# Two-layer expert MLP: the last weight loads swapped and cut into pieces, the last two experts' layers interleaved

## The chip, the cores and the metric

The kernel runs on one core of a Trainium2 chip. The metric is the device time of one execution in microseconds (us). The profiler's page gives, beside it, the span of the profiled execution, from the first to the last recorded instruction; it is about 2 us shorter than the device time. Every time below that is taken from inside the execution counts from the start of that span.

## The reference

Eight experts each apply two matrix products with a ReLU between them to their own 256 tokens. All inputs and the output are float32.

```python
n_experts, capacity, hidden, expert_hidden = 8, 256, 512, 2048
# x  [8, 256, 512]   w1 [8, 512, 2048]   w2 [8, 2048, 512]
h = np.matmul(x, w1)
h = np.maximum(h, 0)
return np.matmul(h, w2).astype(np.float32)
```

One expert's w1 and its w2 are 4 MB each in float32, x is 0.5 MB, the output 0.5 MB.

## The kernel before, in words

The kernel goes through the experts e = 0 to 7 (line 93). For each one it has the following parts.

Loads: `load_x` (lines 57 to 60) brings x as float32 over SyncE's queue. `load_w1` (62 to 65) and `load_w2` (67 to 85) bring the weights over GpSimd's queue, and the transfer converts them to bfloat16, so each weight takes 2 MB in SBUF. w2 of expert 7 comes in six pieces, in units of one 128-row block: 4, 4, 4, 2, 1 and 1 (line 77). All other weights are one DMA each. The order on GpSimd's queue is w1 of 0, w2 of 0, w1 of 1, w2 of 1 and so on (lines 89 to 96). A load may be issued as soon as its buffer is free: w1 has four buffers (line 45), w2 four (line 46), x three (line 42).

Preparation: VectorE casts x to bfloat16 (line 101), TensorE transposes it in eight 128 by 128 blocks into one PSUM tile (line 105), and VectorE copies that to `xT` (line 107).

Layer 1: 64 matmuls of 128x128 by 128x256 (line 119). Eight of them fill one PSUM tile `h_ps`, of which there are four (line 50), and ScalarE applies the ReLU on the way to `hT` in bfloat16 (line 126). There are two `hT` buffers (line 47).

Layer 2: 32 matmuls of 128x128 by 128x512 (line 140) into two PSUM tiles `o_ps`, one for each half of the tokens. For experts 0 to 6 all 16 blocks k of the first half come before those of the second (line 138). For expert 7 the two halves alternate at each k (line 136), so that the matmuls can follow the pieces of w2 as they land. VectorE copies the result to SBUF (line 151; for the second half of expert 7 ScalarE does, line 149), and SyncE's queue stores it (line 156; lines 153 and 154 for expert 7, one store per half, on SyncE's and ScalarE's queue).

The order on each engine is chosen by a scheduler from the program and its dependences. On TensorE it came out as: layer 1 of e, layer 2 of e, transposes of e + 1, layer 1 of e + 1.

Of the kernel before, what the change touches and what calls it, by code (L numbers as in the profile page):

```python
# [1 line left out]

# [5 lines left out]

FP32 = mybir.dt.float32  # L10
BF16 = mybir.dt.bfloat16

J = 16


@with_exitstack
def kernel(
    ctx: ExitStack,  # L20
    tc: tile.TileContext,
    x: bass.AP,
    w1: bass.AP,
    w2: bass.AP,
    out: bass.AP,
):
    nc = tc.nc
    P = 128
    E, C, H = x.shape
    F = w1.shape[2]  # L30
    MC = C // P
    K1 = H // P
    K2 = F // P
    NB = K2 // J

    x_v = x.rearrange("e (p mo) k -> e p (mo k)", mo=MC)
    out_v = out.rearrange("e (p mo) k -> e p (mo k)", mo=MC)
    w1_v = w1.rearrange("e (p ko) n -> e p (ko n)", ko=K1)
    w2_v = w2.rearrange("e (b p j) n -> e p b (j n)", p=P, j=J)

    const = ctx.enter_context(tc.tile_pool(name="const", bufs=1))
    x_pool = ctx.enter_context(tc.tile_pool(name="x_pool", bufs=3))
    xb_pool = ctx.enter_context(tc.tile_pool(name="xb_pool", bufs=2))
    xT_pool = ctx.enter_context(tc.tile_pool(name="xT_pool", bufs=2))
    w1_pool = ctx.enter_context(tc.tile_pool(name="w1_pool", bufs=4))
    w2_pool = ctx.enter_context(tc.tile_pool(name="w2_pool", bufs=4))
    hT_pool = ctx.enter_context(tc.tile_pool(name="hT_pool", bufs=2))
    out_pool = ctx.enter_context(tc.tile_pool(name="out_pool", bufs=3))
    psum_t = ctx.enter_context(tc.tile_pool(name="psum_t", bufs=1, space=bass.MemoryType.PSUM))
    psum_h = ctx.enter_context(tc.tile_pool(name="psum_h", bufs=4, space=bass.MemoryType.PSUM))  # L50
    psum_o = ctx.enter_context(tc.tile_pool(name="psum_o", bufs=3, space=bass.MemoryType.PSUM))

    identity = const.tile([P, P], BF16, name="identity")

    xs, w1s, w2s = {}, {}, {}

    def load_x(e):
        t = x_pool.tile([P, MC * H], FP32, name="x_sb")
        nc.sync.dma_start(t[:], x_v[e])
        xs[e] = t  # L60

    def load_w1(e):
        t = w1_pool.tile([P, K1 * F], BF16, name="w1_sb")
        nc.gpsimd.dma_start(t[:], w1_v[e])  # L64
        w1s[e] = t

    def load_w2(e):

        t = w2_pool.tile([P, NB, J * H], BF16, name="w2_sb")
        w2s[e] = []  # L70
        if e < E - 1:
            nc.gpsimd.dma_start(t[:], w2_v[e])  # L72
            for b in range(NB):
                for j in range(J):
                    w2s[e].append(t[:, b, j * H:(j + 1) * H])
        else:
            pieces = [4, 4, 4, 2, 1, 1]
            k = 0
            for i, n in enumerate(pieces):
                b, j = divmod(k, J)  # L80
                c = w2_pool.tile([P, n * H], BF16, name=f"w2_last{i}", bufs=1)
                nc.gpsimd.dma_start(c[:], w2_v[e, :, b, j * H:(j + n) * H])  # L82
                for q in range(n):
                    w2s[e].append(c[:, q * H:(q + 1) * H])
                k += n

    load_x(0)
    load_x(1)
    load_w1(0)
    make_identity(nc, identity)  # L90
    load_w2(0)

    for e in range(E):
        if e + 1 < E:
            load_w1(e + 1)
            load_w2(e + 1)
        if e + 2 < E:
            load_x(e + 2)

        xb = xb_pool.tile([P, MC, P, K1], BF16, name="xb")  # L100
        nc.vector.tensor_copy(xb[:].rearrange("p m q k -> p (m q k)"), xs[e][:])  # L101
        xt_ps = psum_t.tile([P, K1, MC, P], BF16, name="xt_ps")
        for ko in range(K1):
            for mo in range(MC):
                nc.tensor.transpose(xt_ps[:, ko, mo, :], xb[:, mo, :, ko], identity[:])  # L105
        xT = xT_pool.tile([P, K1, C], BF16, name="xT")
        nc.vector.tensor_copy(  # L107
            xT[:].rearrange("p k c -> p (k c)"),
            xt_ps[:].rearrange("p k m q -> p (k m q)"),
        )  # L110

        w1_r = w1s[e][:].rearrange("p (ko b q j) -> p ko b q j", ko=K1, b=NB, j=J)
        hT = hT_pool.tile([P, K2, C], BF16, name="hT")
        for pr in range(K2 // 2):
            h_ps = psum_h.tile([P, 2, C], FP32, name="h_ps")
            for s in range(2):
                b, j = divmod(pr * 2 + s, J)
                for ko in range(K1):
                    nc.tensor.matmul(  # L119
                        h_ps[:, s, :],  # L120
                        w1_r[:, ko, b, :, j],
                        xT[:, ko, :],
                        start=(ko == 0),
                        stop=(ko == K1 - 1),
                    )
            nc.scalar.activation(  # L126
                hT[:, pr * 2:pr * 2 + 2, :].rearrange("p a c -> p (a c)"),
                h_ps[:].rearrange("p a c -> p (a c)"),
                mybir.ActivationFunctionType.Relu,
            )  # L130

        last = e == E - 1
        out_sb = out_pool.tile([P, MC, H], FP32, name="out_sb")
        o_ps = [psum_o.tile([P, H], FP32, name="o_ps") for _ in range(MC)]
        if last:
            order = [(k, m) for k in range(K2) for m in range(MC)]
        else:
            order = [(k, m) for m in range(MC) for k in range(K2)]
        for k, m in order:
            nc.tensor.matmul(  # L140
                o_ps[m][:],
                hT[:, k, m * P:(m + 1) * P],
                w2s[e][k],
                start=(k == 0),
                stop=(k == K2 - 1),
            )
            if k == K2 - 1:
                if last and m == 1:
                    nc.scalar.copy(out_sb[:, m, :], o_ps[m][:])  # L149
                else:  # L150
                    nc.vector.tensor_copy(out_sb[:, m, :], o_ps[m][:])  # L151
                if last:
                    eng = nc.scalar if m == 1 else nc.sync
                    eng.dma_start(out_v[e, :, m * H:(m + 1) * H], out_sb[:, m, :])
        if not last:
            nc.sync.dma_start(out_v[e], out_sb[:].rearrange("p m h -> p (m h)"))


# [1 line left out]
_INS = ['x', 'w1', 'w2']  # L160
_OUTS = [((8, 256, 512), 'float32')]


# [23 lines left out]
```

## Time and profile before

| What | Value |
|---|---|
| Time, median of three runs | 188.87 us (188.48 to 188.89) |
| Time of the profiled execution | 188.91 us |
| Its span | 186.9 us |
| TensorE: matmuls busy | 131.1 us, 70% of the span |
| TensorE: weight loads into the array | 90.7 us, 49% |
| ScalarE / VectorE / GpSimd busy | 40.1 / 20.2 / 12.4 us |
| Layer 1 matmul (128x256), 512 of them | 293 ns mean of one |
| Layer 2 matmul (128x512), 256 of them | 410 ns mean (379 ns in expert 7) |
| ReLU on ScalarE (128x512), 64 of them | 597 ns |
| Copy of one output half, VectorE | 692 ns |
| Weight DMA of 2 MB in SBUF, issue to landing | 75.7 us median |
| TensorE layer 1 waiting for a weight DMA | 28.3 us, in 7 waits |
| TensorE layer 2 waiting for a weight DMA | 17.2 us, in 7 waits |

Matmuls overlap in TensorE's pipeline, so the mean length of one is more than the distance between two: the 32 matmuls of the last layer 2, of 379 ns each, take 7.07 us together. The time from issue to landing of a weight DMA is mostly time in the queue behind earlier ones. PE in the profile is TensorE, PEld its weight loads, DVE VectorE, ACT ScalarE, POOL GpSimd and SP SyncE; SPq and POOLq are their DMA issues. In the rows of 40 slices, one slice is 4.67 us and a digit is tenths.

### The profile page before, as it was taken

Reading aid. Unit: us, or ns where it says so; the run is one execution under the profiler, and the core shown is the slowest. Engines: PE = TensorE matmul, PEld = TensorE weight load, DVE = VectorE, ACT = ScalarE, POOL = GpSimd, SP = SyncE. Lnnn points to the kernel's source line nnn. Section 1 sums busy time; section 2 is a strip of 40 time slices with the busy share of each in tenths; the row PEclk is TensorE's granted clock in tenths of the full one; section 3 lists DMA queues with packets and bytes.
Section 4 is the critical chain, followed back from the end, with each engine's and each line's share of the span. In section 5 each row is a group of like instructions: output and inputs, shape, how many; then the busy total and the mean of one; then the engine's idle time right before and its main releaser. Section 6 shows DMA issues by size and latency. Waiting matters only on the chain.

```text
span 186.9 us, 1894 instructions
## 1 busy us (share of the span) xinstructions
PE 131.1 (70%) x832; PEld 90.7 (49%) x832; DVE 20.2 (11%) x31; ACT 40.1 (21%) x66; POOL 12.4 (7%) x27
## 2 busy tenths in 40 slices
PE   0204949469593798929779592998778592979990
PEld 0103934249342695428624591347734591339740
DVE  1201001400014000130001400013003000030001
ACT  2000630015300153003600171003600261005501
POOL 7400010100101001010110100001010100000000
PEclk9999999978999589996969997599999999699999
DMA  7989999999999999999999899999999999999902
GB/s 251 239 210 263 228 222 268 211 259 231 221 270 216 248 237 224 267 211 247 243 222 265 200 269 224 226 224 210 250 217 221 239 213 262 214 193 246 214 13 112
DMA packets 5479, 42.05 MB, mean 225 GB/s; under 512 B 608, under 2 KB 864, under 8 KB 3552
## 3 DMA queue, kind: packets, MB, share of 16 engines
q0 software_dynamic: 3024, 33.56, 84.7%
q1 hardware_dynamic: 2304, 8.13, 11.5%
q10 hardware_dynamic: 144, 0.26, 0.4%
q8 instruction: 6, 0.10, 0.2%
q14 instruction: 1, 0.01, 0.0%
HBM read 71.30 MB, written 4.19 MB: 404 GB/s over the span
## 4 chain that ended last, share of the span: by engine, by line
PE 56%; DMA 25%; another core or an unknown queue 14%; POOL 1%; issue 1%; DVE 0%; ACT 0%; POOLq 0%; DVEq 0%
PE o_ps L140 30%; PE h_ps L119 25%; DMA w_sb<-in_w_dram 25%; PE xt_ps L105 1%; POOL w_sb L64 1%; DVE xT L107 0%; ACT out_sb L149 0%; POOL w_sb L72 0%; POOL identity masks.py:199 0%; POOL identity masks.py:197 0%; POOLq masks.py:199 0%; DVE out_sb L151 0%; DVEq L151 0%; DVEq L101 0%
## 5 line engine op out<-in xcount | busy, mean ns | idle before, releaser
L119 PE MATMUL h_ps<-xT,w_sb 128*128 128x256 bf16 x512 | 64.7, 293 | 29.2 <-DMA w_sb<-in_w_dram 28.3
L119 PEld LDWEIGHTS <-w_sb 128*128 128x128 bf16 x512 | 59.8, 147 | 33.6 <-DMA w_sb<-in_w_dram 29.5
L140 PE MATMUL o_ps<-w_sb,hT 128*128 128x512 bf16 x224 | 55.4, 410 | 17.2 <-DMA w_sb<-in_w_dram 17.2
L126 ACT ACTIVATE hT<-h_ps 128x512 bf16<-128x512 f32 x64 | 38.2, 597 | 135.8 <-PE h_ps L119 135.8
L140 PEld LDWEIGHTS <-hT 128*128 128x128 bf16 x256 | 26.4, 103 | 51.3 <-issue 26.5
L151 DVE COPY out_sb<-o_ps 128x512 f32<-128x512 f32 x15 | 10.4, 692 | 147.1 <-PE o_ps L140 147.1
L64 POOL DMA_DIRECT2D w_sb<-in_w_dram x8 | 4.9, 617 | 58.3 <-PE h_ps L119 57.6
L105 PE MATMUL xt_ps<-identity,xb 128*128 128x128 bf16 x64 | 5.3, 230 | 4.8 <-DVE xb L101 4.8
L105 PEld LDWEIGHTS <-xb 128*128 128x128 bf16 x64 | 4.7, 117 | 6.3 <-DVE xb L101 4.7
L101 DVE CAST xb<-x_sb 128x1024 bf16<-128x1024 f32 x8 | 5.5, 687 | 15.5 <-DMA x_sb<-in_x_dram 15.5
L140 PE MATMUL o_ps<-w_last,hT 128*128 128x512 bf16 x32 | 7.1, 379 | 0.0
L82 POOL DMA_DIRECT2D w_last<-in_w_dram x6 | 3.2, 530 | 51.5 <-DMA w_sb<-in_w_dram 51.5
L107 DVE COPY xT<-xt_ps 128x1024 bf16<-128x1024 bf16 x8 | 5.4, 681 | 0.0
L72 POOL DMA_DIRECT2D w_sb<-in_w_dram x7 | 3.7, 534 | 25.1 <-PE o_ps L140 25.1
L149 ACT COPY out_sb<-o_ps 128x512 f32<-128x512 f32 x1 | 0.6, 586 | 6.3 <-PE o_ps L140 6.3
L126 ACT ACT_TABLE_LOAD x1 | 1.3, 1283 | 0.7 <-PEq L171 0.7
masks.py:199 POOL TENSOR_SCALAR_AFFINE_SELECT identity<-identity 128x128 bf16<-128x128 bf16 x1 | 0.3, 314 | 0.1
masks.py:197 POOL MEMSET identity<- 128x128 bf16 x1 | 0.2, 224 | 0.0
L171 POOL MEMSET const-float32-0.0<- 128x1 f32 x1 | 0.1, 99 | 0.2 <-issue 0.2
L171 POOL MEMSET const-bfloat16-1.0<- 128x1 bf16 x1 | 0.1, 103 | 0.0
L171 POOL MEMSET const-uint8-127<- 128x1 uint8 x1 | 0.1, 103 | 0.0
L171 POOL MEMSET const-float32-1.0<- 128x1 f32 x1 | 0.1, 99 | 0.0
## 6 DMA issues: line engine op xcount, KB each, us to landing
w_sb<-in_w_dram POOLq DMA_DIRECT2D x15, 2048.0 KB, 75.7
x_sb<-in_x_dram SPq DMA_DIRECT2D x8, 512.0 KB, 27.9
out_dram<-out_sb SPq DMA_DIRECT2D x7, 512.0 KB, 15.1
w_last<-in_w_dram POOLq DMA_DIRECT2D x3, 512.0 KB, 67.7
w_last<-in_w_dram POOLq DMA_DIRECT2D x1, 256.0 KB, 51.1
w_last<-in_w_dram POOLq DMA_DIRECT2D x2, 128.0 KB, 36.4
out_dram<-out_sb SPq DMA_DIRECT2D x1, 256.0 KB, 2.0
out_dram<-out_sb ACTq DMA_DIRECT2D x1, 256.0 KB, 2.6
```

The lines of the kernel that those rows point to most:

```text
L64: nc.gpsimd.dma_start(t[:], w1_v[e])
L72: nc.gpsimd.dma_start(t[:], w2_v[e])
L82: nc.gpsimd.dma_start(c[:], w2_v[e, :, b, j * H:(j + n) * H])
L101: nc.vector.tensor_copy(xb[:].rearrange("p m q k -> p (m q k)"), xs[e][:])
L105: nc.tensor.transpose(xt_ps[:, ko, mo, :], xb[:, mo, :, ko], identity[:])
L107: nc.vector.tensor_copy(xT[:].rearrange("p k c -> p (k c)"), xt_ps[:].rearrange("p k m q -> p (k m q)"),)
L119: nc.tensor.matmul(h_ps[:, s, :], w1_r[:, ko, b, :, j], xT[:, ko, :], start=(ko == 0), stop=(ko == K1 - 1),)
L126: nc.scalar.activation(hT[:, pr * 2:pr * 2 + 2, :].rearrange("p a c -> p (a c)"), h_ps[:].rearrange("p a c -> p (a c)"), mybir.ActivationF ...
L140: nc.tensor.matmul(o_ps[m][:], hT[:, k, m * P:(m + 1) * P], w2s[e][k], start=(k == 0), stop=(k == K2 - 1),)
L149: nc.scalar.copy(out_sb[:, m, :], o_ps[m][:])
L151: nc.vector.tensor_copy(out_sb[:, m, :], o_ps[m][:])
L171: nc = _bacc.Bacc("TRN2", target_bir_lowering=False, num_devices=1)
```

## The change

The order of the weight loads is a list now, in which w2 of expert 6 and w1 of expert 7 are swapped: the last four weights come as w1 of 6, w1 of 7, w2 of 6, w2 of 7. w2 comes in two halves for experts 0 to 5, in four quarters for expert 6, and in the same six pieces as before for expert 7. The halves have six buffers, that is three experts' worth, where whole w2 tiles had four.

Expert 6's layer 2 alternates the two token halves at each k, as expert 7's did. The loop body is split into `prepare`, `layer1` and `layer2`. The order on TensorE is no longer left to the scheduler but is that of the program: layer 1 of e, transposes of e + 1, layer 2 of e. For expert 6, layer 1 of expert 7 goes between them: layer 1 of 6, transposes of 7, layer 1 of 7, layer 2 of 6, layer 2 of 7. PSUM has three tiles for layer 1 instead of four, and four for layer 2 instead of three.

```diff
-    w2_v = w2.rearrange("e (b p j) n -> e p b (j n)", p=P, j=J)
+    w2_v = w2.rearrange("e (p j) n -> e p (j n)", p=P)
...
-    psum_h = ctx.enter_context(tc.tile_pool(name="psum_h", bufs=4, space=bass.MemoryType.PSUM))
-    psum_o = ctx.enter_context(tc.tile_pool(name="psum_o", bufs=3, space=bass.MemoryType.PSUM))
+    psum_h = ctx.enter_context(tc.tile_pool(name="psum_h", bufs=3, space=bass.MemoryType.PSUM))
+    psum_o = ctx.enter_context(tc.tile_pool(name="psum_o", bufs=4, space=bass.MemoryType.PSUM))
...
+    PIECES = {E - 2: [4, 4, 4, 4], E - 1: [4, 4, 4, 2, 1, 1]}
+    BUFS = {8: 6, 4: 7, 2: 1, 1: 2}
+
     def load_w2(e):
+        w2s[e] = []
+        k = 0
+        for n in PIECES.get(e, [8, 8]):
+            c = w2_pool.tile([P, n * H], BF16, name=f"w2_{n}", bufs=BUFS[n])
+            nc.gpsimd.dma_start(c[:], w2_v[e, :, k * H:(k + n) * H])
...
+    weights = []
+    for e in range(E):
+        weights += [(load_w1, e), (load_w2, e)]
+    weights[-3], weights[-2] = weights[-2], weights[-3]
...
-        if last:
+        if e in PIECES:
             order = [(k, m) for k in range(K2) for m in range(MC)]
...
+    load_x(0)
+    load_x(1)
+    advance(1)
+    make_identity(nc, identity)
+    advance(1)
+    with tc.manual_schedule(engines={mybir.EngineType.PE}):
+        xT = prepare(0)
+        for e in range(E - 1):
+            advance(2)
+            if e + 2 < E:
+                load_x(e + 2)
+            hT = layer1(e, xT)
+            xT = prepare(e + 1)
+            if e == E - 2:
+                hT_last = layer1(E - 1, xT)
+            layer2(e, hT)
+        layer2(E - 1, hT_last)
```

`advance(n)` issues the next n entries of the list of weights. The views of w1 and w2 lose the block index `b`, which had one value only, so each load still fetches the same rows.

## The prediction

> **What bounds the kernel now.** I read the page first, for the limit of the whole, then the chain of waits in order of time, for the end, then the single DMA issues and stretches of 1 us. The page (rows of 40 slices, then the weight queue, then memory traffic):
>
> ```profile
> PEclk9999999978999589996969997599999999699999
> DMA  7989999999999999999999899999999999999902
> ...
> q0 software_dynamic: 3024, 33.56, 84.7%
> ...
> HBM read 71.30 MB, written 4.19 MB: 404 GB/s over the span
> ```
>
> The DMA engines are busy in 38 of 40 slices and stop two slices before the end. The 71.3 MB are x and both weights in float32, each read once, so there is nothing to save there. Up to about 178 us the kernel is a stream of loads with the matmuls waiting beside it; what a change of order can win lies in the last two slices. The chain of waits (start, length, what) shows them:
>
> ```profile
> 146.92 7.21 PE h_ps L119 x64
> 154.13 3.65 another core or an unknown queue
> 157.78 0.04 issue
> 157.82 8.75 PE o_ps L140 x32
> 166.57 0.45 PE xt_ps L105 x8
> 167.02 1.10 another core or an unknown queue
> 168.12 0.04 issue
> 168.17 7.21 PE h_ps L119 x64
> 175.38 6.92 PE o_ps L140 x32
> 182.30 0.02 issue
> 182.32 0.59 ACT out_sb L149
> ```
>
> Each "unknown queue" piece ends where a weight load lands: w1 of expert 6 at 146.9, w2 of 6 at 157.8, w1 of 7 at 168.1. From there 14.13 us of matmuls run without a gap to 182.30, and 4.6 us of copies and stores follow (186.9 - 182.3). The six pieces of the last w2 are not on that path. GpSimd's timeline gives the issue of a piece, the DMA view of that moment its time to landing (last column):
>
> ```profile
> 94.62 0.53 POOL L82 DMA_DIRECT2D w_last<-in_w_dram  x1 [1.63 <-DMA w_sb<-in_w_dram]
> 147.16 0.53 POOL L82 DMA_DIRECT2D w_last<-in_w_dram  x1 [9.70 <-DMA w_sb<-in_w_dram]
> ```
> ```profile
> w_last<-in_w_dram POOLq DMA_DIRECT2D x1, 512.0 KB, 75.4
> w_last<-in_w_dram POOLq DMA_DIRECT2D x1, 128.0 KB, 31.7
> ```
>
> The first piece lands at 94.6 + 75.4 = 170.0, the last at 147.2 + 31.7 = 178.9. Worked the same way the others land at 173.4, 176.2, 177.5 and 178.1. The last matmul pair needs the last piece at about 181.9. So between the end of the loads (178.9) and the end of TensorE (182.3) lie 3.4 us in which only matmuls run: expert 7's two layers, 14.1 us, start 10.8 us before the loads end.
>
> The clock is the second thing to read. In stretches of 1 us (columns: us, PE, PEld, DVE, ACT, POOL busy, granted clock, DMA share, GB/s):
>
> ```profile
> 160.00:161.00 1.00, 1.00 (x4) 0.43 (x3) 0.00 (x0) 0.00 (x0) 0.00 (x0) 0.50 0.84 180
> 163.00:164.00 1.00, 1.00 (x6) 0.45 (x5) 0.69 (x1) 0.00 (x0) 0.00 (x0) 1.00 1.23 262
> ```
>
> Layer 2 of expert 6 ran at half clock from 159 to 162.3 and took 8.75 us instead of 7.07. TensorE's timeline shows when this happens: after idle stretches of 4.24, 4.04, 3.53, 3.53 and 3.69 us the layer took 8.88, 9.66, 8.87, 9.68 and 8.75; after nine shorter ones (0.80 to 2.72) it took 7.07 to 7.21 eight times and 8.64 once (layer 1 of expert 0, after the start, left aside).
>
> [...] 0.50 after every idle stretch of 3.5 to 4.2 us[...]. [...] the last two pieces land 0.6 and 0.8 us after their predecessors. [...] here piece 1 lands 3.4 us after piece 0, with expert 6's store (issued 167.3, landed 175.0) in flight, while piece 0 took 1.9 us from 168.1.
>
> **The change part by part.**
>
> *Swapped loads.* The same bytes on the same GpSimd queue; w1 of 7 takes the place of w2 of 6, so it lands at 157.8 instead of 168.1, and w2 of 6 ends at about 168.2. Issue is early enough: w1 of 7 waits for layer 1 of expert 3 and was issued at 92.5, 75.7 us ahead of its landing. What is queued behind it are the w2 pieces, whose predecessors still have five loads of about 10.8 us outstanding ((168.12 - 16.4)/14 = 10.84 per load). Cost nothing, hidden by those loads.
>
> *Pieces.* w2 becomes 22 DMAs instead of 13 (6x2 + 4 + 6 against 7 + 6), nine more issues of 0.53 us on GpSimd, which otherwise waits (134 us in all), so nothing there. In the built program each weight DMA waits for the eighth before it; seven are then still in flight, and even when the last 128 KB piece is issued these are 2.9 MB of bfloat16 by the sizes in the diff. Per boundary I allow 0 to 0.1 us of lost DMA time, because the six last pieces (168.1 to 178.9, store included, 10.8 us) take no longer than a mean whole load; I take 0. The w2 buffers hold three experts instead of four; w2 of 3 then waits for layer 2 of expert 0 (done near 33 us) with four loads in flight: 0.
>
> *Middle of the kernel.* Layer 2 can start on the first half, about 5 us before the second lands; after that 24 of 32 matmuls remain, 5.3 us instead of 7.07. TensorE thus idles longer before each layer 1: for expert 6 from 142 to 143 until 146.9, so by the pattern above its clock falls and layer 1 of 6 takes 8.9 to 9.7 us, to 155.8-156.6. All of this lies under loads: 0.
>
> *Transposes ahead of layer 2.* The 0.6 us of transposes and 0.68 us copy of expert 7 run after layer 1 of 6 and end by 157.2-158.0, where before the copy ended just ahead of the load (167.9 against 168.1). Takes 0 to 0.15 us at 157.8; I take 0.05. Because of that late layer 1 the idle stretch before layer 1 of 7 is only 0.7 to 1.5 us, so I take full clock for it.
>
> *Interleaved tail.* From 157.87 TensorE has three layers: 7.21 + 6.92 + 6.92 = 21.05, without waits to 178.9. w2 of 6 lands in quarters of about 2.6 us (160.4, 163.0, 165.6, 168.2), while layer 2 of 6 runs 165.1 to 172.0 and needs its last quarter at 170.3: no wait. Layer 2 of 7 (172.0) needs pieces at 172.0, 173.7, 175.4, 177.2, 178.0, 178.5. With the landings of before it would wait for piece 2 (176.2) and end at 176.2 + 16 matmuls of 0.216 = 179.7. But expert 6's store moves from 167.3 to about 173.6; its 0.5 MB, some 1.3 us at the mean 404 GB/s, no longer precedes pieces 1 and 2, only the last ones. Then the last piece at 178.9 and two matmuls (0.43) decide: 179.3. Bounds 178.9 and 179.7; I take 179.3. PSUM for layer 1 goes from four to three buffers: a pair of 8 matmuls lasts 0.88 us, its activation 0.60, so two buffers' worth of time is enough: 0. The last copies and stores are as before, 4.6 us.
>
> *Sum.* 182.3 - 179.3 = 3.0 us. Span 186.9 - 3.0 = 183.9. The profiled execution took 188.91 us, close to the top of the three runs (188.48 to 188.89), so the same 3.0 comes off the median: 185.9 us.
>
> **The rivals.**
>
> *A, the sum above:* 185.9, with 185.0 to 186.8 from the bounds (0.4 each way), a landing of w1 of 7 that moves by 0.3, and the spread of runs. Chance 0.63.
>
> *B, the clock:* layer 1 of 7 begins at half clock, as it would if layer 1 of 6 ran fast and left 3.3 us idle, or as happened once after 2.2 us. Price 1.65 to 2.6 us (8.87 - 7.21; 9.68 - 7.07), all on the path since three layers now follow 157.8 without a gap. TensorE ends at 180.5 to 181.5: 187.1 to 188.1. For it: one cold start in nine short gaps[...]; against: the long layer 1 before it. Chance 0.20.
>
> *C, no gain:* the loads end later by 2.7 to 3.4 us, or w1 of 7 doesn't land before 160.5, because the halves and the earlier x loads (expert 7's activations are fetched about 10 us sooner) rearrange the stream: 188.6 to 189.2. Against: the same bytes precede w1 of 7. Chance 0.08.
>
> *D, slower:* every piece boundary on the GpSimd queue costs DMA time. Nine boundaries more, all ahead of the last landing: from 0.38 us each (3.4/9) the gain is gone; at 0.5 us the loads end 4.5 us later and the time is 188.87 - 3.0 + 4.5 = 190.4[...]. Against: the last two pieces land 0.6 and 0.8 us after their predecessors, and each is 256 KB of float32 in memory, 0.65 us at 404 GB/s, so that nothing is left for a boundary. I leave it 0.09 because no 1 MB piece beside an undivided load is shown.
>
> **How the numbers follow.** Three runs tell apart about 0.2% (0.4 us). A and B lie below 188.5, apart from B's last tenth; with C and D: faster 0.83, within 0.2% 0.08, slower 0.09. The range is A's and B's, 185.0 to 188.1: what is left out is C and D, 0.17, and a few in a hundred below.
>
> **What would show it.** After: w1 of 7's first matmul near 157.9; layer 1 of 7, layer 2 of 6, layer 2 of 7 back to back, full clock from 158 on; TensorE's end near 179.3, within 0.5 us of the last landing; DMA busy as before until 178 to 179. Half clock after 158 shows B, loads that end after 180 show D, a first matmul of layer 1 of 7 after 160 shows C. I would be wrong also if the three layers took the path with waits between them, for w2 quarters landing after 170.3.

## The result

| Kernel | Time, median | Runs | Ratio to before, 95% interval |
|---|---|---|---|
| Before | 188.88 us (188.48 to 189.52) | 4 | |
| Changed | 186.62 us (186.32 to 186.69) | 4 | 0.987 (0.984 to 0.990) |
| Changed, once more beside later runs | 186.57 us (186.34 to 186.84) | 5 | 0.988 (0.985 to 0.990) |

The change makes the kernel 2.3 us faster, where 3.0 was forecast. The profiled execution took 186.69 us, its span is 184.6 us against 186.9: the same 2.3.

### The profile after

The page's rows of 40 slices (now 4.6 us each) and its weight queue (packets, MB, share of the span):

```profile
PEclk9999999966999759997899969997999969999999
DMA  6999999999999999999999999999999999999963
...
q0 software_dynamic: 4320, 33.56, 86.7%
```

The DMA engines are now busy for six tenths of the last slice but one, where they stood at 0 before: nearly all of the stretch at the end in which only matmuls ran is gone. TensorE's timeline (start, length, line, what, and in brackets the idle time before it and what ended it), from layer 1 of expert 6 to the end:

```profile
147.36 8.76 PE L106 MATMUL h_ps<-xT,w_sb 128*128 128x256 bf16 x64 [4.37 <-DMA w_sb<-in_w_dram]
155.96 0.61 PE L90 MATMUL xt_ps<-identity,xb 128*128 128x128 bf16 x8
158.39 7.21 PE L106 MATMUL h_ps<-xT,w_sb 128*128 128x256 bf16 x64 [1.82 <-DMA w_sb<-in_w_dram]
165.44 13.54 PE L129 MATMUL o_ps<-w,hT 128*128 128x512 bf16 x60
179.47 0.59 PE L129 MATMUL o_ps<-w,hT 128*128 128x512 bf16 x2 [0.49 <-DMA w<-in_w_dram]
```

w1 of 7 lands at 158.3 instead of 168.1. Layer 1 of 6 is slow (8.76 us, granted clock 0.50 from 147.2 to 150.6) after 4.4 us of idleness, layer 1 of 7 is at full speed (7.21, clock 1.00) after 1.8, and the two layers 2 follow without a gap. The last two matmuls wait 0.5 us for the last piece of w2. The chain of waits ends the same way:

```profile
163.53 15.91 DMA w<-in_w_dram
179.43 0.04 issue
179.47 0.61 PE o_ps L129 x2
180.08 0.02 issue
180.10 0.59 ACT out_sb L138
```

So TensorE ends at 180.1 instead of 182.3, and a load is the last thing that it waits for. What follows takes 4.5 us, as before (4.6).

### The profile page after: what moved, and what is told of

Read it like the earlier page. It is cut to its first block, busy times and chain, and to the rows that moved or that the text cites. A ratio compares the mean times of both kernels' runs of the same rounds, so it can differ in the third digit from the quotient of the medians.

```text
span 184.6 us, 1897 instructions
## 1 busy us (share of the span) xinstructions
PE 130.5 (71%) x824; PEld 91.7 (50%) x832; DVE 20.8 (11%) x31; ACT 40.1 (22%) x66; POOL 17.6 (10%) x36
## 3 DMA queue, kind: packets, MB, share of 16 engines
q0 software_dynamic: 4320, 33.56, 86.7%
## 4 chain that ended last, share of the span: by engine, by line
another core or an unknown queue 42%; DMA 35%; PE 11%; POOL 6%; issue 4%; ACT 0%; POOLq 0%
DMA w<-in_w_dram 35%; PE o_ps L129 6%; PE h_ps L106 5%; POOL w L73 4%; POOL w_sb L62 1%; ACT out_sb L138 0%; PE xt_ps L90 0%; POOL identity masks.py:199 0%; POOL identity masks.py:197 0%; POOLq masks.py:199 0%; POOLq L195 0%; POOLq L62 0%; POOLq L73 0%; POOLq L184 0%
## 5 line engine op out<-in xcount | busy, mean ns | idle before, releaser
L106 PE MATMUL h_ps<-xT,w_sb 128*128 128x256 bf16 x512 | 70.6, 309 | 41.4 <-DMA w_sb<-in_w_dram 41.4
L106 PEld LDWEIGHTS <-w_sb 128*128 128x128 bf16 x512 | 62.9, 149 | 50.6 <-DMA w_sb<-in_w_dram 44.8
L129 PE MATMUL o_ps<-w,hT 128*128 128x512 bf16 x248 | 56.9, 379 | 3.2 <-DMA w<-in_w_dram 2.7
L129 PEld LDWEIGHTS <-hT 128*128 128x128 bf16 x256 | 24.8, 98 | 32.3 <-issue 4.5
L73 POOL DMA_DIRECT2D w<-in_w_dram x22 | 12.5, 568 | 119.0 <-DMA w_sb<-in_w_dram 67.9
L62 POOL DMA_DIRECT2D w_sb<-in_w_dram x8 | 4.6, 570 | 27.1 <-DMA w<-in_w_dram 26.3
## 6 DMA issues: line engine op xcount, KB each, us to landing
out_dram<-out_sb SPq DMA_DIRECT2D x7, 512.0 KB, 10.8
```

Of the source, the lines that this page charges most:

```text
L73: nc.gpsimd.dma_start(c[:], w2_v[e, :, k * H:(k + n) * H])
L106: nc.tensor.matmul(h_ps[:, s, :], w1_r[:, ko, :, j], xT[:, ko, :], start=(ko == 0), stop=(ko == K1 - 1),)
L129: nc.tensor.matmul(o_ps[m][:], hT[:, k, m * P:(m + 1) * P], w2s[e][k], start=(k == 0), stop=(k == K2 - 1),)
```

## The experiments

My theory was that the gain is TensorE's tail, that it takes the swap, the interleaving and the pieces together, and that the clock of layer 1 of 7 is what endangers it. The rivals: the pieces alone or the fixed order make it; the new DMAs cost time of their own. Every ratio is to runs of the kernel before on the same chip. Interleaving without the swap was not run, nor the swap with whole w2 tiles only.

### Loads swapped, layers not interleaved

```diff
             xT = prepare(e + 1)
-            if e == E - 2:
-                hT_last = layer1(E - 1, xT)
             layer2(e, hT)
-        layer2(E - 1, hT_last)
+        layer2(E - 1, layer1(E - 1, xT))
```

> The changed kernel with the loads swapped and w2 in pieces, but with layer 2 of expert 6 ahead of layer 1 of expert 7 on TensorE. My theory (swap, pieces and interleaving only pay together): layer 2 of 6 can't end before its last quarter (168.2) and 8 matmuls, 169.9; then layer 1 of 7 (7.2) and layer 2 of 7 (6.9) follow, so TensorE ends near 184.0 instead of 180.1 and the time is about 190.5 us, slower than before. Rival (the gain comes from the pieces, or from the transposes and the fixed order on TensorE, which all stay in): about 186.6 us.

Measured: 190.7 us, ratio 1.009 (1.007 to 1.011). TensorE's timeline at its end:

```profile
168.00 1.89 PE L129 MATMUL o_ps<-w,hT 128*128 128x512 bf16 x8 [0.35 <-DMA w<-in_w_dram]
169.72 7.15 PE L106 MATMUL h_ps<-xT,w_sb 128*128 128x256 bf16 x64
176.71 7.07 PE L129 MATMUL o_ps<-w,hT 128*128 128x512 bf16 x31
```

The last quarter of w2 of 6 lands at 168.0, its 8 matmuls take to 169.7, and two whole layers remain. w1 of 7 had been there for more than ten microseconds. As long as TensorE doesn't use that weight when it comes, the swap gains nothing: these 8 matmuls now stand between the landing near 168 and expert 7's two layers, and the kernel is 1.7 us slower than before.

### Pieces and fixed order alone

The same edit, and the swap taken out:

```diff
-    weights[-3], weights[-2] = weights[-2], weights[-3]
```

> The changed kernel with the loads in their old order and without interleaving; the pieces and the fixed order on TensorE stay. My theory: w1 of 7 lands near 168.6 as before; layer 2 of 6 has followed its quarters and ended by 160.2, so TensorE idles over 8 us, begins layer 1 of 7 at half clock (8.9 to 9.7 us instead of 7.2), and ends at 184.4 to 185.2: 190.8 to 191.7 us, slower than before. Rival (pieces, or the fixed order, make the gain): 186.6 to 187.5 us.

Measured: 190.49 us (188.75 to 191.87, 20 runs), ratio 1.007 (1.005 to 1.009).

```profile
156.45 7.07 PE L128 MATMUL o_ps<-w,hT 128*128 128x512 bf16 x31
168.07 8.88 PE L105 MATMUL h_ps<-xT,w_sb 128*128 128x256 bf16 x64 [4.55 <-DMA w_sb<-in_w_dram]
176.79 7.07 PE L128 MATMUL o_ps<-w,hT 128*128 128x512 bf16 x31
```

Pieces alone make it slower, and through the clock: layer 2 of 6 is done early, TensorE idles for 4.55 us, and layer 1 of 7 takes 8.88 us instead of 7.21, on the path. (A layer 1 of 8.87 us in the trace of the kernel before, at 83.3, had the clock at 0.50 for 3.41 us.) I had expected 8 us of idleness; layer 2 of 6 could not start until layer 1 of 6 and the transposes had ended at 156.4, which I had left out. The layer's price was at the low end of what I had expected (8.9 to 9.7 us), and the time 0.3 us below it. The fixed order on TensorE stays in here too, and makes no gain that shows.

### w2 of expert 6 in one piece

```diff
-    PIECES = {E - 2: [4, 4, 4, 4], E - 1: [4, 4, 4, 2, 1, 1]}
-    BUFS = {8: 6, 4: 7, 2: 1, 1: 2}
+    PIECES = {E - 2: [16], E - 1: [4, 4, 4, 2, 1, 1]}
+    BUFS = {16: 1, 8: 6, 4: 3, 2: 1, 1: 2}
```

> The changed kernel with w2 of expert 6 in one DMA instead of four. My theory: layer 2 of 6 can't start before the whole w2 has landed (168.2) instead of at 165.4, so TensorE ends at 168.2 + 13.9 = 182.1, two us later: 188.6 us at full clock, up to 190.3 if the 2.8 us of idleness halve the clock. Rival (only the last piece of w2 of 7 sets the end, so the quarters do nothing): 186.6 us.

Measured: 190.15 us, ratio 1.003 (1.001 to 1.005). Of 20 runs 7 lie at 188.4 to 188.7 and 13 at 190.0 to 190.3, the two values expected. The profiled execution (188.66 us) has both layers 2 at full speed, 62 matmuls in 13.97 us:

```profile
168.08 13.97 PE L129 MATMUL o_ps<-w,hT 128*128 128x512 bf16 x62 [2.17 <-DMA w<-in_w_dram]
```

In it TensorE ends at 182.1 instead of 180.1, since its last 13.97 us start at 168.1: the quarters are worth these two microseconds. That the upper group is the half clock after 2 to 3 us of idleness is argued from its distance, 1.65 us, and not shown by a trace; the last section shows how such a stretch can go either way.

### Work in the idle stretch before layer 1 of expert 6

```diff
+            if e == E - 2:
+                fill_ps = psum_o.tile([P, H], FP32, name="o_ps")
+                for k in range(16):
+                    nc.tensor.matmul(fill_ps[:], hT[:, k, 0:P], w2s[e - 1][k], start=(k == 0), stop=(k == 16 - 1))
             hT = layer1(e, xT)
```

> The changed kernel with 16 more matmuls of 128x512, whose result nobody uses, on TensorE between layer 2 of expert 5 and layer 1 of expert 6, where it idles for 4.4 us. My theory (idleness before layer 1 of 6 makes it slow, and its late end keeps the clock up for layer 1 of 7): layer 1 of 6 now takes 7.2 us and ends near 154.6, TensorE idles 3.7 us until w1 of 7 lands, and layer 1 of 7 takes 8.9 to 9.7 us; TensorE ends at 181.1 to 182: 187.6 to 188.6 us. Rival (the clock of layer 1 of 7 doesn't hang on what ran before): 186.6 us, layer 1 of 7 in 7.2 us.

Measured: 187.41 us (186.61 to 187.59), ratio 0.989 (0.983 to 0.994), 0.8 us above the changed kernel.

```profile
147.22 7.21 PE L106 MATMUL h_ps<-xT,w_sb 128*128 128x256 bf16 x64 [0.50 <-DMA w_sb<-in_w_dram]
154.27 0.61 PE L90 MATMUL xt_ps<-identity,xb 128*128 128x128 bf16 x8
158.26 8.87 PE L106 MATMUL h_ps<-xT,w_sb 128*128 128x256 bf16 x64 [3.38 <-DMA w_sb<-in_w_dram]
166.97 13.98 PE L129 MATMUL o_ps<-w,hT 128*128 128x512 bf16 x62
```

With the idle stretch filled, layer 1 of 6 takes 7.21 us, ends early, and the idleness moves to the place ahead of layer 1 of 7, which now takes 8.87. More work for TensorE before the tail made the layer fast that didn't matter and slow the one that did. Of the 1.66 us only 0.9 reach TensorE's end (181.0 against 180.1), because the wait at the end is gone: the last piece landed at 178.1. That left the time 0.2 us below what I had expected. This is the step of the prediction that I trusted least, and it holds.

### w2 of experts 0 to 5 whole

```diff
-        for n in PIECES.get(e, [8, 8]):
+        for n in PIECES.get(e, [16]):
```

with `BUFS = {16: 3, 4: 7, 2: 1, 1: 2}`.

> The changed kernel with w2 of experts 0 to 5 in one DMA each (three buffers, so as much memory as the halves). My theory: the halves matter for the clock alone. Layer 2 of expert 5 now ends near 144.4, about 1.5 us later, TensorE idles 2.9 us instead of 4.4 before layer 1 of 6; if that layer then runs at full clock, it ends at 154.6, the idle stretch before layer 1 of 7 is 3.7 us, and that layer takes 1.7 us longer: 187.6 us. If 2.9 us is enough to halve the clock, nothing changes: 186.6 us. Rival (boundaries cost 0.06 us each, six fewer): 186.2 us, with the loads ending at 179.1.

Measured: 186.8 us, ratio 0.988 (0.984 to 0.991); its four runs are 186.29, 186.41, 187.19 and 187.20, and the profiled one is the slowest of these.

```profile
146.94 7.21 PE L106 MATMUL h_ps<-xT,w_sb 128*128 128x256 bf16 x64 [2.85 <-DMA w_sb<-in_w_dram]
153.99 0.61 PE L90 MATMUL xt_ps<-identity,xb 128*128 128x128 bf16 x8
157.84 8.88 PE L106 MATMUL h_ps<-xT,w_sb 128*128 128x256 bf16 x64 [3.24 <-DMA w_sb<-in_w_dram]
166.56 13.98 PE L129 MATMUL o_ps<-w,hT 128*128 128x512 bf16 x64
```

Both the theory and the rival are in it. After only 2.85 us of idleness layer 1 of 6 ran fast and layer 1 of 7 slow, as in the run before. But w1 of 6 and of 7 landed 0.4 and 0.5 us sooner than in the changed kernel (146.9 and 157.8 against 147.3 and 158.3), at the moments of the kernel before. With six DMAs fewer the stream is half a microsecond earlier. The 1.67 us of clock, less 0.55 for the sooner load and 0.5 of wait that falls away at the end, leave 0.6; TensorE ended 0.5 us later than in the changed kernel. The last piece landed at 177.7, where the rival had 179.1; expert 6's store was issued 1.1 us later here (174.8 against 173.6), and what that does to the last landing is the subject of the experiment after the next.

### w2 of experts 0 to 5 in eight pieces, and in four

```diff
-        for n in PIECES.get(e, [8, 8]):
+        for n in PIECES.get(e, [2] * 8):
```

(and `[4] * 4`, each with as many buffers as three experts need).

> The changed kernel with w2 of experts 0 to 5 in eight pieces each instead of two, 36 DMAs more. My theory (boundaries between queued DMAs cost nothing; the last load landed 0.6 us later than before for another reason): loads end at 179.4 as now, 186.6 us. Rival (each boundary costs what the nine new ones would have to cost if they made the loads end 0.6 us later, 0.06 us): 36 x 0.06 = 2.2 us more, w1 of 7 lands near 160.5, 188.8 us.

> The changed kernel with w2 of experts 0 to 5 in four pieces each instead of two, 12 DMAs more. My theory now (each further DMA in the stream costs about 0.06 us, from 36 of them that cost 2.1): w1 of 7 lands near 159.1, the last piece 0.7 us later than in the changed kernel: 187.3 us. Rival (nine new DMAs cost nothing[...]): 186.6 us.

Measured: 188.59 us in eight pieces, ratio 0.998 (0.997 to 0.999), and 187.57 us in four, ratio 0.993 (0.991 to 0.996), where the changed kernel beside the latter took 186.57. The weight queue in eight pieces, then in four:

```profile
q0 software_dynamic: 9504, 33.56, 89.7%
```
```profile
q0 software_dynamic: 6048, 33.56, 87.9%
```

Each DMA brings 144 packets, whatever its size (9504/66, 6048/42, 4320/30, 3024/21). The queue's packets took 167.6 us on each DMA engine in eight pieces (89.7% of 186.8), 162.8 in four, 160.0 in two and 158.3 in the kernel before: about 0.2 us for each further DMA. The stream is delayed by less, so most of that time lies beside other packets: w1 of 7 lands at 160.5 in eight pieces (36 DMAs more than in two, 2.1 us), at 158.8 in four (12 more, 0.45 us), at 158.3 in two, at 157.8 whole (six fewer, 0.5 us), so 0.04 to 0.09 us for each. The rival of the first run, 188.8 us, was right within 0.2. The loads of x and the stores don't explain the half microsecond of the changed kernel: by 147 us SyncE's queue had moved the same 6.82 MB in it and in the kernel before. But the number of DMAs, the length of their rows and the bytes that the DMAs in flight hold change together here, so a cost for each DMA is the simplest reading, not one that is shown against the others.

In four pieces the last piece landed at 179.3, no later than in two, so the 0.7 us that I expected there are not what made it slower, and that the time came near my 187.3 is in part luck. Expert 6's store was issued 0.9 us later (174.5) and landed after the last piece (180.0), which may have made up for the further DMAs. In its profiled execution layer 1 of 6 took 9.99 us, and layer 1 of 7 had to wait for its transposed x until 159.3; TensorE ended 0.2 us later than in the changed kernel, and the stretch after it was longer by 0.4, for which the trace shows no cause.

### Expert 6's store behind the last pieces

The last piece, of 128 KB in SBUF, landed 2.0 us after the one before it. GpSimd's timeline, then the DMA view of the two issues, then that of expert 6's store, which was issued at 173.6, in the changed kernel:

```profile
161.05 0.53 POOL L73 DMA_DIRECT2D w<-in_w_dram  x1 [1.89 <-DMA w<-in_w_dram]
163.53 0.53 POOL L73 DMA_DIRECT2D w<-in_w_dram  x1 [1.95 <-DMA w<-in_w_dram]
```
```profile
w<-in_w_dram POOLq DMA_DIRECT2D x1, 128.0 KB, 16.4
w<-in_w_dram POOLq DMA_DIRECT2D x1, 128.0 KB, 15.9
```
```profile
out_dram<-out_sb SPq DMA_DIRECT2D x1, 512.0 KB, 6.0
```

161.05 + 16.4 = 177.5, 163.53 + 15.9 = 179.4, and the store lands at 179.6: all of it fell on the end of the stream. From 173 to 180 SyncE's queue moved its 0.52 MB, beside 0.77 MB on the weight queue. The experiment puts that store on GpSimd's queue, which the weights use:

```diff
-            nc.sync.dma_start(out_v[e], out_sb[:].rearrange("p m h -> p (m h)"))
+            eng = nc.gpsimd if e == E - 2 else nc.sync
+            eng.dma_start(out_v[e], out_sb[:].rearrange("p m h -> p (m h)"))
```

> The changed kernel with expert 6's store on GpSimd's queue, behind the last pieces of w2, instead of SyncE's. My theory (that store, issued at 173.6 and landed at 179.6, took turns with the last two pieces and stretched them): the last piece lands near 178.1 instead of 179.4, TensorE's last two layers run without a wait and end at 179.3 to 179.4 instead of 180.1: 185.9 us. Rival (the loads ended late for another reason, or a queue's order doesn't keep the store behind the pieces): 186.6 us, last piece still near 179.4.

Measured: 185.65 us, ratio 0.983 (0.980 to 0.986).

```profile
158.25 7.21 PE L106 MATMUL h_ps<-xT,w_sb 128*128 128x256 bf16 x64 [1.80 <-DMA w_sb<-in_w_dram]
165.30 13.98 PE L129 MATMUL o_ps<-w,hT 128*128 128x512 bf16 x64
...
173.78 0.54 POOL L146 DMA_DIRECT2D out_dram<-out_sb  x1 [9.87 <-DVE out_sb L140]
```

The 64 matmuls of both layers 2 run to 179.3 without a wait; the last piece lands at 178.0 (issued at 163.4, 14.6 us to landing), 0.7 us after the one before it instead of 2.0, and the store at 179.2, behind the pieces. The run with the filled idle stretch agrees: with the same DMAs, and the store issued 1.5 us later (175.2), its last piece landed at 178.1. So the store in flight cost the last piece 1.4 us, and behind the pieces it does no harm. The span fell by 1.2 us, of which TensorE's end explains 0.8. The rest is after TensorE's end and stays open: that stretch is 4.1 to 4.2 us in all four kernels with this store on GpSimd's queue, and 4.5 to 4.9 in the others.

### Three versions that go on from there

All three keep the store on GpSimd's queue. First, w1 of 6 and of 7 ahead of w2 of 5, so that three layers no longer follow one landing:

```diff
-    weights[-3], weights[-2] = weights[-2], weights[-3]
+    weights[-5:-1] = [(load_w1, E - 2), (load_w1, E - 1), (load_w2, E - 3), (load_w2, E - 2)]
...
-        for e in range(E - 1):
+        for e in range(E - 3):
...
+        hs = []
+        for e in range(E - 3, E):
+            hs.append(layer1(e, xT))
+            if e + 1 < E:
+                xT = prepare(e + 1)
+        for e in range(E - 3, E):
+            layer2(e, hs[e - E + 3])
```

> As the run with the store on GpSimd's queue, and w1 of 6 and 7 loaded ahead of w2 of 5, with the last three experts' layers 1 ahead of their layers 2 (three hT buffers, five half buffers of w2). My theory (with three layers no longer following one landing, only the last piece sets the end): w1 of 7 lands near 147.4, layer 2 of 5 and of 6 follow their pieces, layer 2 of 7 ends two matmuls after the last piece, 178.1 + 0.5 = 178.6 instead of 180.1: 185.1 us. Rival (TensorE's own chain of layers still decides): no faster than 185.9 us.

Measured: 185.42 us, ratio 0.982 (0.979 to 0.985), not to be told from the run before it. TensorE now follows the pieces:

```profile
170.44 1.90 PE L129 MATMUL o_ps<-w,hT 128*128 128x512 bf16 x8 [0.89 <-DMA w<-in_w_dram]
173.03 1.89 PE L129 MATMUL o_ps<-w,hT 128*128 128x512 bf16 x8 [0.69 <-DMA w<-in_w_dram]
175.47 3.61 PE L129 MATMUL o_ps<-w,hT 128*128 128x512 bf16 x16 [0.55 <-DMA w<-in_w_dram]
```

The last wait ends at 175.5 and 16 matmuls remain, so TensorE ended at 179.1. I had named the very last piece (178.0); the third one decided.

Second, fewer DMAs as well, with the buffers cut to make room:

```diff
-    PIECES = {E - 2: [4, 4, 4, 4], E - 1: [4, 4, 4, 2, 1, 1]}
+    PIECES = {E - 2: [8, 4, 4], E - 1: [4, 4, 2, 2, 2, 1, 1]}
+    BUFS = {16: 2, 8: 3, 4: 4, 2: 3, 1: 2}
...
-    w1_pool = ctx.enter_context(tc.tile_pool(name="w1_pool", bufs=4))
+    w1_pool = ctx.enter_context(tc.tile_pool(name="w1_pool", bufs=3))
```

> As the run with w1 of 6 and 7 ahead of w2 of 5, with 25 weight DMAs instead of 30: w2 of experts 0 to 4 whole (two buffers, and three of w1), of 6 in pieces of 8, 4 and 4, of 7 in 4, 4, 2, 2, 2, 1 and 1. My theory (0.06 us for each DMA saved, 0.3 us; and no wait for a large piece near the end, where the run before waited for the third piece of w2 of 7 at 175.5 and then needed 3.6 us): last piece near 177.7, TensorE ends near 178.2 instead of 179.1: 184.5 us. Rival (the end of TensorE is not what its last wait suggests, or fewer buffers stall the queue): 185.4 us or more.

Measured: 198.2 us, ratio 1.050 (1.047 to 1.053), far slower.

```profile
92.42 0.53 POOL L62 DMA_DIRECT2D w_sb<-in_w_dram  x1 [12.29 <-PE h_ps L106]
92.94 1.70 POOL L73 DMA_DIRECT2D w<-in_w_dram  x3
122.39 0.53 POOL L62 DMA_DIRECT2D w_sb<-in_w_dram  x1 [27.75 <-PE h_ps L106]
```

The third line is w1 of 7. With three buffers it waited for layer 1 of 4, until 122.4, and three w2 pieces had gone into the queue ahead of it; it landed at 161.5 instead of 147.2, with three layers 2 behind it on TensorE. Layer 1 of 4 was late itself: layer 2 of 3 ahead of it had waited 12.9 us, until 105.5, for its w2. This run says nothing on the number of DMAs.

Third, only the finer end, with four w1 buffers and halves for experts 0 to 5: the `PIECES` of the run before, and `BUFS = {8: 6, 4: 4, 2: 3, 1: 2}`.

> As the run with w1 of 6 and 7 ahead of w2 of 5 (six half buffers, four of w1), but with w2 of 6 in pieces of 8, 4 and 4 and w2 of 7 in 4, 4, 2, 2, 2, 1 and 1, the same 30 weight DMAs. My theory (there layer 2 of 7 waited for the third piece at 175.5 and then needed 16 matmuls, 3.6 us): pieces of two blocks land every 1.2 us from 174.2 on, the last near 178.0, TensorE ends two matmuls later, near 178.5 instead of 179.1: 184.9 us. Rival (the end hangs on TensorE's chain, not on the size of the pieces): 185.4 us.

Measured: 184.96 us (184.92 to 185.19, 6 runs), ratio 0.979 (0.976 to 0.981). TensorE ended at 178.8. Its last long wait is for the second piece, at 173.1, with 24 matmuls behind it; the chain of waits shows one more, too short for the timeline, for the third piece of two blocks:

```profile
157.63 19.16 DMA w<-in_w_dram
176.79 0.04 issue
176.83 1.95 PE o_ps L129 x8
```

So again a piece with matmuls behind it decided, 8 of them now, and not the last one (178.1), which I had named. This is the fastest version, 3.9 us under the kernel before, and its interval lies below that of the changed kernel, though not below those of the runs at 185.65 and 185.42 us.

The changed kernel itself, beside two of these runs, is the third row of the first table.

> The changed kernel once more, beside the other two: 186.6 us by every theory.

## Why the prediction was right, and by how much it was off

*The bound and the place of the gain.* Right. The loads still fill the DMA engines (90% or more in 37 of 40 slices), and the gain comes from the end, where only matmuls ran. Leaving out a part takes it away: 190.7 without interleaving, 190.5 without swap and interleaving, 188.5 or 190.2 without quarters.

*Swapped loads.* w1 of 7 landed at 158.3, forecast 157.8: off by 0.5, for the reason that follows.

*Pieces: "I take 0."* This is a term that was mis-sized. With each further DMA in the queue w1 of 7 landed 0.04 to 0.09 us later, inside the bound that I gave (0 to 0.1), but not nothing: with six more ahead of it, 0.5 us. Rival D has a price for each DMA, which is the simplest reading of the runs, but its 0.38 us are six times the 0.06 us that they give; by the prediction's own sum the gain was gone from 3.0/9 = 0.33 us.

*Middle of the kernel, and the clock of layer 1 of 7.* The mechanism is right, and the filled idle stretch shows it (layer 1 of 6 in 7.21 us after 0.50 us of idleness, layer 1 of 7 in 8.87 after 3.38). Both sizes lie just outside the forecast: 8.76 us for layer 1 of 6 (8.9 to 9.7) and 1.8 us of idleness after it (0.7 to 1.5); layer 1 of 7 took 7.21 us all the same. None of the nine runs (186.3 to 186.8) shows the price of the half clock. The shortest idle stretch ahead of a slow layer was 2.22 us in the kernel before and 4.05 in the changed one; how near 1.8 us came to it is not shown. Rival B is what the changed kernel becomes when layer 1 of 6 is made fast, at the price forecast (8.87 us), though only 0.8 us of it reached the median, mostly because the wait at the end falls away. (In the kernel before, the half clock of layer 2 of 6 lasted to 162.5, not 162.3.) The transposes ahead of layer 2 and the three PSUM tiles cost nothing, as forecast.

*Interleaved tail.* The mechanism was right: the last piece and two matmuls decide. The size was off: last piece at 179.4 instead of 178.9. I had moved expert 6's store away from pieces 1 and 2, rightly (the seven pieces before the small ones landed 2.4 us apart, 160.8 to 175.5), but kept the last landing where it was, and it came 0.55 us later. The store's size was right: 1.3 us forecast, and 1.4 us is what its absence gives. But in the kernel before it had also landed ahead of the last piece (175.0), so its new place does not explain the 0.55. The stream was late by 0.5 at w1 of 7 already, which points to the further DMAs; that is argued, and no run separates it here. The run with the store behind the pieces took the wait away. The two matmuls and the start after the landing took 0.65 us, where I had 0.43.

*Sum.* TensorE's end moved by 182.3 - 180.1 = 2.2 us instead of 3.0. The missing 0.8 are the last landing (0.55) and what follows it (0.2).

*Rival C* (loads later by 2.7 us or more) did not occur; half a microsecond of it did.

## What to carry to other kernels

When a kernel is a stream of loads, look at what compute is left after the last one: order the loads so that the weights with the most work behind them come first, and let the compute take them in that order; the loads reordered alone cost time here. Count what else is in flight at the end, a store on another queue too, and size the last pieces so that no large one has more matmuls behind it than the rest of the stream lasts. When an engine's clock falls after idleness, as it did here (0.50 after 4.4 us), ask in which layer the idle stretch lies, not how long it is in all.

## What the runs showed of the hardware that I had not expected

The smaller the pieces of w2 on GpSimd's queue were, the sooner the transfers on SyncE's landed. The x loads of 512 KB on SyncE's queue took a median of 27.9 us from issue to landing before, and in the changed kernel and with eight pieces:

```profile
x_sb<-in_x_dram SPq DMA_DIRECT2D x8, 512.0 KB, 16.5
```
```profile
x_sb<-in_x_dram SPq DMA_DIRECT2D x8, 512.0 KB, 12.8
```

The stores of 512 KB went the same way, 15.1, 10.8 and 6.8 us. Why is not shown: no run separates the length of the weights' rows from the number of DMAs. The weights moved too: w1 of 1 landed at 39.2 with whole w2 tiles, 40.7 with halves and 43.1 with eighths, long before the kernel had issued many of its additional DMAs, when more of x had gone ahead of it: by 20 us SyncE's queue had moved 1.75, 1.90 and 2.40 MB.

By length alone it looks like chance whether an idle stretch of 2 to 4 us halves the clock. In the kernel before, 2.2 us was once enough (8.64 us for the layer 2 at 94.4, clock 0.50 from 94.2 to 97.6), while with the filled idle stretch and with eight pieces a layer 1 took 7.21 us after 3.86 and 3.81 us; in the run with whole w2 one layer took 7.07 us after 3.23 us, and another 8.88 after 3.24. The traces show one thing more. In those of the kernel before and of the changed kernel, every stretch of half or full clock between two changes lasted 3.41 us or a whole multiple of it (from 3.41 to 37.55 us, within 0.02). Here is the run with whole w2, cut into parts of that length (columns as in the prediction):

```profile
131.96:135.37 3.41, 1.84 (x21) 1.72 (x20) 0.69 (x1) 1.47 (x3) 0.00 (x0) 1.00 1.07 257
135.37:138.79 3.42, 1.76 (x9) 0.81 (x9) 0.00 (x0) 0.00 (x0) 0.53 (x1) 1.00 0.98 224
...
155.85:159.27 3.42, 1.43 (x13) 1.43 (x14) 0.00 (x0) 0.23 (x1) 0.53 (x1) 1.00 1.03 228
159.27:162.68 3.41, 3.41 (x18) 2.71 (x17) 0.00 (x0) 1.56 (x3) 0.53 (x1) 0.50 1.07 216
```

The idle stretch of 3.23 us (133.8 to 137.0) falls into two parts, in which matmuls fill 54% and 51%, and the clock stays at 1.00. That of 3.24 us (154.6 to 157.8) leaves one part with 1.43 of 3.42 us, 42%, and the next one is at 0.50. In the kernel before, the 2.2 us left one part with 1.38 of 3.41 us, 40% (90.8 to 94.2), and the next was at 0.50. In the changed kernel, the 1.8 us ahead of layer 1 of 7 fall into two parts with 74% and 73% (154.0 to 160.9), and the clock stays at 1.00. So in these four cases the clock went with how busy the matmuls were in such a part, where the length of the idle stretch does not tell them apart.
